# Gate and up by Strassen's algorithm in two token halves, and linear attention in 64-column tiles

## The chip, the cores and the metric

The kernel runs on one core of one Trainium2 chip. The metric is the device time of one launch in microseconds (us). In the profile PE is the matrix engine (TensorE) and PEld its weight loads, DVE is VectorE, ACT is ScalarE, POOL is GpSimd, and SP issues the DMAs. PSUM is the memory that PE writes its sums to, in banks; SBUF is the memory in which all engines' tiles lie.

## The reference

One decoder layer and a last norm, over 1024 prompt tokens and 64 sample tokens (1088 together), model width 1024 and a feed-forward width of 2816, all in float32:

```python
def decoder_layer(x, s0, k_buf, v_buf, w_in, w_gup, b_g, g_mix, g_gla, w_out,
                  g_ffn, w_fg, w_fu, w_fd):
...
    mix = jnp.concatenate([o_g, o_s.reshape(B, T, -1).astype(x.dtype)], axis=-1) @ w_out
    h = x + mix
    hn = rmsnorm(h, g_ffn)
    y = h + (jax.nn.silu(hn @ w_fg) * (hn @ w_fu)) @ w_fd
```

o_g comes from four heads of gated linear attention, chunk after chunk with a state S (64x128 per head). o_s comes from eight heads of dilated windowed attention. y then gets a last rmsnorm.

## The kernel before, in words

Every large product is made from float32 operands that are split in two (L171 on ACT makes the high part, L172 on DVE the low part: raw minus high). One product is then three matmuls per 128x128 block of weights: high by high, high by low, low by high (mm3, L200 to L202). Activations lie transposed, features on the 128 partitions and tokens along the row, and the 1088 tokens are worked on in three chunks, CHUNKS, of 384, 384 and 320. So nearly all of PE's work is matmuls of 128x128 weights by 384 or 320 columns.

The program is ordered by a scheduler: weight loads and their splits are marked high priority and go ahead on their engines, everything else stands where the code puts it. Each engine takes its own instructions strictly in order.

In the order of time: the mixing norm, the input projection with both kinds of attention beside it (0 to about 712 us in the profile), the second half of the out-projection (rows 512 on of `w_out`, the windowed heads; to about 778 us), the feed-forward part (to about 1571 us), and the last norm and output.

- Linear attention: two heads lie in one tile. For each 128 tokens and each head, one matmul makes A by V (L665) and a second adds decayed query by state S (L668). The second has 64 rows of weights, as a head's state is 64 wide.
- Out-projection, second half: `os` loads the attention output of a chunk, 512 rows, from DRAM in one DMA (oraw), and ACT and DVE split it. For each of eight output tiles f and three chunks: the residual with the first half's sum (xa) comes from DRAM, 12 matmuls, an add on DVE into h, a split of h times the norm's gain into hhi and hlo, a square on ACT and a sum on POOL (L1032).
- The norm: the squares are summed over partitions by matmuls with one column (L1038), DVE makes 1/sqrt by small instructions, and it is spread to `rstd_bc` by transposes (L1043 to L1048). Gate and up don't wait for it: `rstd_bc` is multiplied in after their matmuls (L1066, L1068).
- Feed-forward: 22 tiles f of 128 columns. `ff_up(f)` loads and splits 512 KB of gate and of up weights, and for each chunk makes 24 matmuls for gate and 24 for up; DVE, ACT (Silu, L1067), DVE, POOL (L1069) and the split of L171/L172 make ghi and glo. `ff_down` runs once for two tiles f: for each chunk and each of eight output tiles k, 6 matmuls and an add on DVE into h (L1090). So PE makes 3168 matmuls for gate and up, 1584 for down, and 288 for the out-projection's half.
- The tail (L1095 on): the last `ff_down` of each chunk, then transposes, squares, 1/sqrt, and the rows y go out.

Of the kernel before, what the change touches and what calls it, by code (L numbers as in the profile page):

```python
# [102 lines left out]
def hymba_layer(  # L103
# [1103 lines left out]
```

## Time and profile before

| | us |
|---|---|
| runs without the profiler: 1588.16, 1580.25, 1589.38; median | 1588.16 |
| the profiled execution | 1588.28 |
| its span, first to last instruction | 1586.4 |
| PE busy | 1522.2 |
| DVE busy | 717.3 |
| ACT busy | 435.6 |
| POOL busy | 272.1 |

A span is what the profiler saw between the first and the last instruction; 1.9 us of the execution lie around it. An engine is busy while one of its instructions runs. Matmuls overlap in the pipeline, so what one costs is read from the distance between the starts of two of them, and not from its own duration.

### The profile page before, as it was taken

The numbers are of one execution on the slowest core, as the hardware profiler recorded it, in microseconds if no ns is written. First come the engines' busy times: TensorE is split into PE (matmuls) and PEld (weight loads), VectorE is DVE, ScalarE is ACT, GpSimd is POOL, SyncE is SP. The second block draws the span as 40 slices with busy tenths as digits, with TensorE's granted clock in tenths as the row PEclk, the third lists the DMA queues.
The fourth block names the chain that finished last, engine by engine and source line by source line (L and its number), as shares of the span: only waits on it lengthen the run. The fifth ranks groups of instructions, "written<-read, shape, count | busy, mean of one in ns | idle before, by whom it ended". The sixth has DMA issues, their size and how long they took to land.

```text
span 1586.4 us, 28631 instructions
## 1 busy us (share of the span) xinstructions
PE 1522.2 (96%) x12080; PEld 1377.2 (87%) x12080; DVE 717.3 (45%) x1556; ACT 435.6 (27%) x867; POOL 272.1 (17%) x296
## 2 busy tenths in 40 slices
PE   7979999999999998997999999999999999999997
PEld 6768877887776765767999999999999999999997
DVE  5486575543323233335643443433443343444437
ACT  4143242144342445314421212121111212121113
POOL 1494342042112010002310001010000001010002
PEclk9988999999999999989999999999999999999998
DMA  5320121163443547545321101110211101120102
GB/s 155 92 78 30 30 69 43 41 188 106 136 112 93 153 118 217 177 138 175 92 74 50 54 27 54 41 54 27 67 40 41 54 27 54 40 63 18 54 1 114
DMA packets 177425, 126.73 MB, mean 80 GB/s; under 512 B 14576, under 2 KB 169104, under 8 KB 177296
## 3 DMA queue, kind: packets, MB, share of 16 engines
q1 hardware_dynamic: 173088, 124.69, 26.4%
q8 instruction: 95, 1.56, 0.4%
q10 hardware_dynamic: 4208, 0.21, 0.2%
q14 instruction: 34, 0.28, 0.1%
HBM read 101.40 MB, written 23.46 MB: 79 GB/s over the span
## 4 chain that ended last, share of the span: by engine, by line
PE 86%; DMA 5%; DVE 5%; POOL 1%; issue 1%; ACT 1%; SPq 0%; DVEq 0%; ACTq 0%; POOLq 0%
PE ps_mm L200 13%; PE ps_mm L201 12%; PE ps_mm L202 12%; PE ps_S L202 5%; PE ps_S L201 5%; PE ps_S L200 5%; PE ps_T L201 2%; PE ps_T L200 2%; PE ps_T L202 2%; PE ps_S L835 2%; DMA oraw<-o_dram 2%; PE ps_T L933 2%; PE ps_X L977 2%; PE ps_A L202 1%; PE ps_A L200 1%; PE ps_A L201 1%
## 5 line engine op out<-in xcount | busy, mean ns | idle before, releaser
L200 PE MATMUL ps_mm<-xhi,whi 128*128 128x384 f32 (+1 forms) x576 | 199.5, 347 | 2.0 <-ACT whi L171 1.6
L202 PE MATMUL ps_mm<-xhi,wlo 128*128 128x384 f32 (+1 forms) x576 | 194.6, 339 | 1.1 <-DVE wlo L172 1.1
L201 PE MATMUL ps_mm<-xlo,whi 128*128 128x384 f32 (+1 forms) x576 | 194.8, 339 | 0.2 <-DVE xlo L277 0.2
L1069 POOL TENSOR_TENSOR gt<-gt,ut 128x384 f32<-128x384 f32 (+1 forms) x66 | 64.9, 984 | 698.1 <-DVE ut L1068 698.1
L200 PE MATMUL ps_mm<-hhi,whi 128*128 128x384 f32 (+1 forms) x528 | 172.8, 327 | 1.2 <-DVE gt L1066 1.2
L202 PE MATMUL ps_mm<-hhi,wlo 128*128 128x384 f32 (+1 forms) x528 | 173.0, 328 | 0.0
L201 PE MATMUL ps_mm<-hlo,whi 128*128 128x384 f32 (+1 forms) x528 | 172.8, 327 | 0.0
L200 PE MATMUL ps_S<-hhi,whi 128*128 128x384 f32 (+1 forms) x528 | 172.7, 327 | 0.0
L201 PE MATMUL ps_S<-hlo,whi 128*128 128x384 f32 (+1 forms) x528 | 172.7, 327 | 0.0
L202 PE MATMUL ps_S<-hhi,wlo 128*128 128x384 f32 (+1 forms) x528 | 172.5, 327 | 0.0
L200 PEld LDWEIGHTS ps_mm<-xhi,whi 128*128 128x128 f32 x576 | 110.2, 192 | 13.6 <-issue 7.6
L202 PEld LDWEIGHTS ps_mm<-xhi,wlo 128*128 128x128 f32 x576 | 110.2, 191 | 7.3 <-issue 4.8
L201 PEld LDWEIGHTS ps_mm<-xlo,whi 128*128 128x128 f32 x576 | 110.4, 192 | 5.5 <-issue 4.0
L1067 ACT ACTIVATE gt<-gt 128x384 f32<-128x384 f32 (+1 forms) x66 | 33.1, 502 | 294.6 <-DVE gt L1066 294.6
L1068 DVE TENSOR_TENSOR ut<-ps_S,rstd_bc 128x384 f32<-128x384 f32 (+1 forms) x66 | 35.4, 536 | 159.7 <-PE ps_S L202 159.7
L200 PEld LDWEIGHTS ps_mm<-hhi,whi 128*128 128x128 f32 x528 | 99.2, 188 | 1.4 <-DVE gt L1066 1.4
L201 PEld LDWEIGHTS ps_S<-hlo,whi 128*128 128x128 f32 x528 | 99.2, 188 | 0.0
L202 PEld LDWEIGHTS ps_mm<-hhi,wlo 128*128 128x128 f32 x528 | 99.2, 188 | 0.0
L202 PEld LDWEIGHTS ps_S<-hhi,wlo 128*128 128x128 f32 x528 | 99.2, 188 | 0.0
L200 PEld LDWEIGHTS ps_S<-hhi,whi 128*128 128x128 f32 x528 | 99.2, 188 | 0.0
L201 PEld LDWEIGHTS ps_mm<-hlo,whi 128*128 128x128 f32 x528 | 99.2, 188 | 0.0
L1090 DVE TENSOR_TENSOR h<-h,ps_T 128x384 f32<-128x384 f32 (+1 forms) x120 | 63.5, 529 | 68.1 <-PE ps_T L202 68.1
(335 smaller groups left out, 3048.4 us busy)
## 6 DMA issues: line engine op xcount, KB each, us to landing
wraw<-in_w_in_dram SPq DMA_DIRECT2D x22, 512.0 KB, 3.8
wraw<-in_w_ffn_gate_dram SPq DMA_DIRECT2D x22, 512.0 KB, 3.7
wd_raw<-in_w_ffn_down_dram SPq DMA_DIRECT2D x22, 512.0 KB, 3.2
wuraw<-in_w_ffn_up_dram SPq DMA_DIRECT2D x22, 512.0 KB, 3.7
raw<-in_cache_swa_k_dram SPq DMA_DIRECT2D x32, 256.0 KB, 5.4
raw<-in_cache_swa_v_dram SPq DMA_DIRECT2D x32, 256.0 KB, 4.4
xa<-x_dram SPq DMA_DIRECT2D x32, 192.0 KB, 2.6
xr<-in_x_prompt_dram SPq DMA_DIRECT2D x8, 512.0 KB, 8.4
```

The lines of the kernel that those rows point to most:

```text
L200: mm(out=ps, lhsT=whi[k], rhs=xhi[k], start=first and k == 0, stop=False)
L201: mm(out=ps, lhsT=whi[k], rhs=xlo[k], start=False, stop=False)
L202: mm(out=ps, lhsT=wlo[k], rhs=xhi[k], start=False, stop=last and k == n - 1)
L835: ins = mm(out=out, lhsT=qres[own, qi * P + 32 * r : qi * P + 32 * r + 32], rhs=rhs, start=True, stop=True)
L933: nc.tensor.transpose(out=ps[:, r * P : (r + 1) * P], in_=raw[:, r, :], identity=ident)
L977: mm(out=av[rs, b2 * P : (b2 + 1) * P], lhsT=pT[:, t, rs], rhs=vts[b2][:, r, :], start=False, stop=t == 5 and b2 == 1)
L1067: act(out=gt, in_=gt, func=AF.Silu)
L1068: vec.tensor_tensor(out=ut, in0=pu[:, :n], in1=rstd_bc[:, cs], op=ALU.mult)
L1069: pool.tensor_tensor(out=gt, in0=gt, in1=ut, op=ALU.mult)
L1090: vec.tensor_tensor(out=h[:, k, cs], in0=h[:, k, cs], in1=ps[:, :n], op=ALU.add)
```

## The change

Four things change.

1. In linear attention the matmuls of L665 and L668 are cut into 64-column tiles: four for A by V, then four for query by state, where there were two and two, in an order in which neighbours use other parts of the array.
2. The out-projection's second half runs in two token halves of 544, each in two blocks of NH = 272 columns. The first half's h stays in SBUF; the second half's is added into xa and stored back to DRAM, to be read again later. After each half come the sums and `rstd_bc` as before (`out_half`).
3. Gate and up are made by the Strassen-Winograd scheme. The contraction (1024) and the output columns are each cut in two, the tokens of a half too, and seven block products M1 to M7 stand where a plain product has eight. Operands for it: `norm_half` normalises x (now with `rstd_bc` multiplied in first), POOL makes four differences T of 272 columns for each of four pairs of feature tiles, and x blocks and T are split (`operand`). Of the weights POOL makes the four sums S1 to S4, 128x1024 each, and seven blocks are split where there were four. The weights of each pair of f tiles are loaded twice, once per token half. After the products DVE adds the parts together (`after`), and ACT and POOL or DVE make Silu times up.
4. Down stays plain, in blocks of 272 with adds of 544 columns on DVE. The first token half's final rows (five tiles of up to 128 tokens) are made while the second half's first pair is under way (`final_rows`), and then the second half's h is loaded. The tail is cut in 224 and 320 tokens.

PE now makes 3696 matmuls for gate and up, 2112 for down and 384 for the out-projection, nearly all of 272 columns.

```diff
@@ gla head, per chunk @@
+                    os_ = [bank("AX"[i])[:, :P] for i in range(2)]
                     for i in range(2):
-                        o = bank("AX"[i])[:, :P]
-                        hs = slice(64 * i, 64 * i + 64)
-                        mm(out=o, lhsT=AT[:, i * ncmb + c, :], rhs=V[part][:, c, i * P : (i + 1) * P],
-                           start=True, stop=S is None)
-                        if S is not None:
-                            mm(out=o, lhsT=qE[hs, c * P : c * P + P], rhs=S[hs, :], start=False, stop=True)
+                        for ts in halves:
+                            mm(out=os_[i][ts], lhsT=AT[:, i * ncmb + c, ts], rhs=V[part][:, c, i * P : (i + 1) * P],
+                               start=True, stop=S is None)
+                    for ts in halves if S is not None else ():
+                        for i, hs in enumerate(halves):
+                            mm(out=os_[i][ts], lhsT=qE[hs, c * P + ts.start : c * P + ts.stop], rhs=S[hs, :], start=False, stop=True)
+                    for i, o in enumerate(os_):
@@ out-projection, second half, and norm @@
+NH = TT // 4
...
+    def load_rows(c0):
+        hi = outp.tile([P, 4, NH], F32R, tag="ohi", name="ohi", bufs=4)
+        lo = outp.tile([P, 4, NH], F32R, tag="olo", name="olo", bufs=4)
+        for k in range(0, 4, 2):
+            oraw = outp.tile([P, 2, NH], F32, tag="oraw", name="oraw", bufs=3)
+            dma(out=oraw, in_=o_dram[512 + k * P : 512 + (k + 2) * P, c0 : c0 + NH].rearrange("(k p) t -> p k t", p=P))
+            split(hi[:, k : k + 2], lo[:, k : k + 2], oraw)
+        return [hi[:, k] for k in range(4)], [lo[:, k] for k in range(4)]
+    def out_half(hf):
+        os = [load_rows(2 * NH * hf + NH * n) for n in range(2)]
+        sq_acc = outp.tile([P, 2 * NH], F32, tag="acc", name="acc", bufs=2)
+        for f in range(KT):
+            if f % 2 == 0:
+                ws = load_w_out(f, 1)
+            for n in range(2):
+                cs = slice(NH * n, NH * n + NH)
+                xs = x_dram[:, f, 2 * NH * hf + NH * n : 2 * NH * hf + NH * n + NH]
+                xa = outp.tile([P, NH], F32, tag="xa", name="xa", bufs=3)
+                dma(out=xa, in_=xs)
+                ps = bank("mm")[:, :NH]
+                mm3(ps, ws[f % 2], os[n])
+                row = xa if hf else h[0][:, f, cs]
+                vec.tensor_tensor(out=row, in0=ps, in1=xa, op=ALU.add)
+                if hf:
+                    dma(out=xs, in_=xa)
+                if f == 0:
+                    act(out=sq_acc[:, cs], in_=row, func=AF.Square)
+                else:
+                    sq = outp.tile([P, NH], F32, tag="sq", name="sq", bufs=2)
+                    act(out=sq, in_=row, func=AF.Square)
+                    pool.tensor_tensor(out=sq_acc[:, cs], in0=sq_acc[:, cs], in1=sq, op=ALU.add)
...
@@ gate and up @@
+    ORDER = (("M1", "A11", 0, "a", True), ("M6", "S2", 4, "b", True), ("M5", "S1", 3, "c", True), ("M7", "S3", 5, "b", False),
+             ("M2", "A12", 1, "a", False), ("M3", "S4", 2, "c", False), ("M4", "A22", 6, "b", False))
+    def blocks(src, w):
+        raw = {}
+        turn = [0]
+        def room(name):
+            t = raw[name] = ffp.tile([P, KT * P], F32, tag="raw", name="raw", bufs=7)[:, :w]
...
+        for name, m, k in (("A11", 0, 0), ("A21", 1, 0), ("A22", 1, 1), ("A12", 0, 1)):
+            src(room(name), m, k)
+        add = lambda out, a, b, op: pool.tensor_tensor(out=out, in0=raw[a], in1=raw[b], op=op)
+        add(room("S1"), "A21", "A22", ALU.add)
+        add(raw["A21"], "A11", "A21", ALU.subtract)
+        raw["S3"] = raw["A21"]
+        add(room("S2"), "S1", "A11", ALU.subtract)
...
+            if name == "S4":
+                add(raw["S2"], "A12", "S2", ALU.subtract)
+                raw["S4"] = raw["S2"]
...
+        for name, block, slot, bk, first in ORDER:
+            with tc.high_priority():
+                hi, lo = (view(part) for part in parts(block))
+            if bk not in banks:
+                banks[bk] = psum2.tile([P, 2, 512], F32, tag=bk, name=f"ps_{bk}", bufs=2 if bk == "b" else 1)[:, :, :NH]
+            for s in range(2):
+                for k in range(nk):
+                    xhi, xlo = x(k, slot)
+                    one = lambda l, r, i: mm(out=banks[bk][:, s], lhsT=l[:, k, s], rhs=r, start=first and k == 0 and i == 0,
+                                             stop=k == nk - 1 and i == 2, skip_group_check=not first)
+                    one(hi, xhi, 0)
+                    one(hi, xlo, 1)
+                    one(lo, xhi, 2)
+            after(name, banks)
...
+    def operand(pl, B, tag):
+        t = ffp.tile([P, 4, NH], F32, tag="T", name="T", bufs=1)
+        sub = lambda out, a, b: pool.tensor_tensor(out=out, in0=a, in1=b, op=ALU.subtract)
+        sub(t[:, 0], B[:, 3], B[:, 0])
+        sub(t[:, 2], B[:, 2], B[:, 3])
+        sub(t[:, 1], B[:, 2], t[:, 0])
+        sub(t[:, 3], B[:, 1], t[:, 1])
+        hi, lo = (pl.tile([P, 7, NH], F32R, tag=f"{tag}{part}", name=f"{tag}{part}", bufs=4 if tag == "x" else 3) for part in ("hi", "lo"))
+        split(hi[:, 0:3], lo[:, 0:3], B[:, 0:3])
+        split(hi[:, 3:7], lo[:, 3:7], t)
+        return hi, lo
+    def norm_half(hf):
+        t0 = 2 * NH * hf
+        xs = []
+        for k in range(0, KT, 2):
+            B = new_block()
+            for j, v in ((0, B[:, 0:4:3]), (1, B[:, 1:3])):
+                if hf:
+                    dma(out=v, in_=x_dram[:, k + j, t0 : t0 + 2 * NH].rearrange("p (n t) -> p n t", t=NH))
+                vec.scalar_tensor_tensor(
+                    out=v, in0=v if hf else h[0][:, k + j].rearrange("p (n t) -> p n t", t=NH), scalar=gf[:, k + j : k + j + 1],
+                    in1=rstd_bc[:, t0 : t0 + 2 * NH].rearrange("p (n t) -> p n t", t=NH), op0=ALU.mult, op1=ALU.mult)
+            xs.append(operand(bx, B, "x"))
+        return xs
...
+        def made(slot, c, eng):
+            act(out=B[:, slot], in_=c[:, 0], func=AF.Silu)
+            eng.tensor_tensor(out=B[:, slot], in0=B[:, slot], in1=c[:, 1], op=ALU.mult)
+        def after(name, ps):
+            add = lambda out, a, b: vec.tensor_tensor(out=out, in0=a, in1=ps[b], op=ALU.add)
+            if name == "M1":
+                act(out=s1, in_=ps["a"], func=AF.Copy)
+            elif name == "M6":
+                add(u2, s1, "b")
+            elif name == "M5":
+                add(v5, s1, "c")
+            elif name == "M7":
+                add(v5, v5, "b")
+                made(2, v5, pool)
+            elif name == "M2":
+                made(0, ps["a"], vec)
+            elif name == "M3":
+                add(u2, u2, "c")
...
+                add(s1, s1, "b")
+                made(1, s1, pool)
...
@@ down, rows, main loop @@
+    def down(ws, g, h):
+        for k in range(KT):
+            ks = slice(k * P, k * P + P)
+            tag = "abcb"[k % 4]
+            ps = psum2.tile([P, 2, 512], F32, tag=tag, name="ps_d", bufs=2 if tag == "b" else 1)[:, :, :NH]
+            for n in range(2):
+                mm3(ps[:, n], [[w[part][:, ks] for w in ws] for part in range(2)],
+                    [[part[:, j, n * NH : n * NH + NH] for j in range(2)] for part in g])
+            hk = h[:, k].rearrange("p (n t) -> p n t", t=NH)
+            vec.tensor_tensor(out=hk, in0=hk, in1=ps, op=ALU.add)
...
+        ps = psum2.tile([P, 2, 512], F32, tag="b", name="ps_y", bufs=2)
+        y = wpool.tile([P, KT, P], F32, tag="wraw", name="y", bufs=1).rearrange("p (f k) c -> p f (k c)", f=2)
+        c0 = t0 - 2 * NH * hf
+        for k in range(KT):
+            nc.tensor.transpose(out=ps[:m, k // 4, k % 4 * P : k % 4 * P + P], in_=h[hf][:, k, c0 : c0 + m], identity=ident)
+        act(out=y[:m], in_=ps[:m], func=AF.Square, accum_out=st[:m, 0:1])
+        rms(st[:, 1:2], st[:, 0:1], D, st[:, 2:3])
+        vec.scalar_tensor_tensor(out=y[:m], in0=ps[:m], scalar=st[:m, 1:2], in1=gfin[:m].rearrange("p (f c) -> p f c", f=2),
+                                 op0=ALU.mult, op1=ALU.mult)
+        dma(out=out_rows(t0, m), in_=y[:m].rearrange("p f c -> p (f c)"))
...
+    g = None
+    for hf in range(2):
+        for i in range(NF // 2):
+            B = gate_up(i, xs)
+            before, g = g, plain(B)
+            if hf == 0 and i == NF // 2 - 1:
+                xs = norm_half(1)
+            if before:
+                down(ws, before, h[hf])
+            ws = load_down(i)
+            if hf == 0 and i == NF // 2 - 1:
+                down(ws, g, h[0])
+                g = None
+            if hf and i == 0:
+                for t0 in range(0, 2 * NH, P):
+                    final_rows(0, t0, min(P, 2 * NH - t0))
+                h[1] = residual()
+                dma(out=h[1], in_=x_dram[:, :, 2 * NH :])
```

How instructions stand now, at two places. The first is DVE in the feed-forward part. Before, for one pair of tiles f (a weight split is `wlo`, an add after down is L1090):

```order
L1066 TENSOR_TENSOR gt<-ps_mm,rstd_bc 128x320
L172 TENSOR_TENSOR wlo<-wraw,whi 128x1024
L1068 TENSOR_TENSOR ut<-ps_S,rstd_bc 128x320
L172 TENSOR_TENSOR wlo<-wuraw,whi 128x1024
L1090 TENSOR_TENSOR h<-h,ps_T 128x384
L172 TENSOR_TENSOR glo<-gt,ghi 128x320
L172 TENSOR_TENSOR wdlo<-wd_raw,wdhi 128x1024
L1066 TENSOR_TENSOR gt<-ps_mm,rstd_bc 128x384
L1068 TENSOR_TENSOR ut<-ps_S,rstd_bc 128x384
L172 TENSOR_TENSOR glo<-gt,ghi 128x384
```

After, from the last add of one pair's Strassen products (s) to the next pair's first (u), line numbers of the changed kernel (L173 is the low split, L1186 the adds of `after`, L1235 those of `down`):

```order
L1186 TENSOR_TENSOR s_9930<-s_9930,ps_b 128x544
L173 TENSOR_TENSOR glo<-B,ghi 128x544
L173 TENSOR_TENSOR wlo<-raw,whi 128x1024
L1235 TENSOR_TENSOR h<-h,ps_d 128x544 x3
L173 TENSOR_TENSOR glo<-B,ghi 128x544
L1235 TENSOR_TENSOR h<-h,ps_d 128x544 x5
L173 TENSOR_TENSOR wdlo<-raw,wdhi 128x1024 x2
L173 TENSOR_TENSOR wlo<-raw,whi 128x1024
L1186 TENSOR_TENSOR u_10296<-s_10295,ps_b 128x544
L173 TENSOR_TENSOR wlo<-raw,whi 128x1024
```

Before, a pair of f tiles has six weight splits and multiplies and adds in chunks; now three weight splits of the next pair, the split of g and the adds of down stand between the last add of one pair and the first of the next.

The second place is POOL between the out-projection and the first pair of tiles f. Before:

```order
L1032 TENSOR_TENSOR acc<-acc,sq 128x384 x2
L1032 TENSOR_TENSOR acc<-acc,sq 128x320
L1069 TENSOR_TENSOR gt<-gt,ut 128x384 x2
L1069 TENSOR_TENSOR gt<-gt,ut 128x320
L1069 TENSOR_TENSOR gt<-gt,ut 128x384 x2
```

After, from the first half's last sum of squares on (L1053 the sums, L1146 the differences T, L1092 the weight sums S):

```order
L1146 TENSOR_TENSOR T<-B 128x272 x2
L1146 TENSOR_TENSOR T<-B,T 128x272 x2
L1053 TENSOR_TENSOR acc<-acc,sq 128x272 x3
L1146 TENSOR_TENSOR T<-B 128x272 x2
L1053 TENSOR_TENSOR acc<-acc,sq 128x272
L1146 TENSOR_TENSOR T<-B,T 128x272
L1053 TENSOR_TENSOR acc<-acc,sq 128x272 x2
L1146 TENSOR_TENSOR T<-B,T 128x272
L1053 TENSOR_TENSOR acc<-acc,sq 128x272 x3
L1146 TENSOR_TENSOR T<-B 128x272 x2
L1146 TENSOR_TENSOR T<-B,T 128x272
L1092 TENSOR_TENSOR raw<-raw 128x1024
```

The differences of the first half's x, which its products wait for, alternate with the second half's sums of squares, and a weight sum stands between the last of them.

## Rows read from the trace of the kernel before

**Rows 1.** The page: busy us of each engine, share of the span, instructions.

```profile
PE 1522.2 (96%) x12080; PEld 1377.2 (87%) x12080; DVE 717.3 (45%) x1556; ACT 435.6 (27%) x867; POOL 272.1 (17%) x296
```

**Rows 2.** Windows: length, busy us (instructions) of PE, PEld, DVE, ACT, POOL; clock, DMA share, GB/s.

```profile
800.00:900.00 100.00, 100.00 (x612) 100.00 (x611) 40.35 (x65) 20.14 (x31) 10.65 (x10) 1.00 0.15 45
...
720.00:730.00 10.00, 3.27 (x18) 2.94 (x18) 4.14 (x9) 3.77 (x9) 0.00 (x0) 0.86 0.72 236
730.00:740.00 10.00, 10.00 (x51) 10.00 (x52) 4.97 (x11) 4.20 (x10) 1.25 (x2) 0.80 0.16 45
...
780.00:790.00 10.00, 8.54 (x55) 7.92 (x55) 6.58 (x21) 1.05 (x3) 0.00 (x0) 1.00 0.18 52
```

**Rows 3.** Timeline, PE: start us, duration us; ends of two runs of equal matmuls.

```profile
995.51 0.34 PE L202 MATMUL ps_A<-ghi,wdlo 128*128 128x384 f32 x1
...
1013.96 0.33 PE L202 MATMUL ps_X<-ghi,wdlo 128*128 128x384 f32 x1
...
1059.62 0.31 PE L200 MATMUL ps_mm<-hhi,whi 128*128 128x320 f32 x1
...
1066.51 0.31 PE L202 MATMUL ps_S<-hhi,wlo 128*128 128x320 f32 x1
```

**Rows 4.** Timeline of weight loads: six for one-column matmuls, and one of the feed-forward part.

```profile
777.91 0.81 PEld L1038 LDWEIGHTS ps_A<-ones,acc 128*128 128x128 f32 x6
...
1113.24 0.19 PEld L201 LDWEIGHTS ps_mm<-hlo,whi 128*128 128x128 f32 x1
```

**Rows 5.** The critical chain, 700 to 800 us: start us, us on the chain, what.

```profile
720.79 8.60 DMA oraw<-o_dram
```

**Rows 6.** Groups by line and shape, 800 to 1500 us: count, busy us, mean ns, idle before.

```profile
L1069 POOL TENSOR_TENSOR gt<-gt,ut 128x384 f32<-128x384 f32 x41 | 41.7, 1016 | 514.3 <-DVE ut L1068 514.3
L1090 DVE TENSOR_TENSOR h<-h,ps_T 128x384 f32<-128x384 f32 x75 | 41.2, 549 | 40.8 <-PE ps_T L202 40.8
L172 DVE TENSOR_TENSOR wlo<-wuraw,whi 128x1024 fp32r<-128x1024 f32 x21 | 32.3, 1540 | 4.6 <-ACT whi L171 4.6
L172 DVE TENSOR_TENSOR wlo<-wraw,whi 128x1024 fp32r<-128x1024 f32 x20 | 24.5, 1225 | 9.0 <-ACT whi L171 9.0
L172 DVE TENSOR_TENSOR glo<-gt,ghi 128x384 fp32r<-128x384 f32 x42 | 23.5, 559 | 72.7 <-ACT ghi L171 72.7
L1090 DVE TENSOR_TENSOR h<-h,ps_T 128x320 f32<-128x320 f32 x36 | 17.6, 488 | 20.5 <-PE ps_T L202 20.5
```

**Rows 7.** One line's instructions, POOL's scaling of weights: ns min/median/max, first and last start.

```profile
L180 POOL TENSOR_TENSOR wraw<-wraw,gm x22: 1897/1899/2155, 6.8 to 513.7; 128x1024 f32<-128x1024 f32 x22
```

**Rows 8.** Timeline of POOL and DVE around 1114 us: a weight split beside a POOL multiply.

```profile
1113.57 0.88 POOL L1069 TENSOR_TENSOR gt<-gt,ut 128x320 f32<-128x320 f32 x1 [5.95 <-DVE ut L1068]
...
1113.86 1.67 DVE L172 TENSOR_TENSOR wlo<-wuraw,whi 128x1024 fp32r<-128x1024 f32 x1 [0.46 <-ACT whi L171]
```

**Rows 9.** Timeline of DVE in the norm: the chain of small instructions to `rstd_bc`.

```profile
782.53 0.17 DVE L161 TENSOR_SCALAR st<-st 128x9 f32<-128x9 f32 x1
782.74 0.17 DVE L152 TENSOR_SCALAR st<-st 128x9 int32<-128x9 int32 x1
...
788.37 1.01 DVE L1066 TENSOR_TENSOR gt<-ps_mm,rstd_bc 128x384 f32<-128x384 f32 x2
```

**Rows 10.** Scaling of the final rows on DVE (512 columns), one line: ns min/median/max.

```profile
L1171 DVE SCALAR_TENSOR_TENSOR y<-ps_S,st,gfin x2: 741/742/743, 1559.3 to 1574.6; 128x512 f32<-128x512 f32 x2
```

**Rows 11.** Squares of the final rows on ACT (512 columns), timeline.

```profile
1563.01 0.59 ACT L1114 ACTIVATE y<-ps_S 128x512 f32<-128x512 f32 x1
```

**Rows 12.** DMA issues: count, KB each, median us from issue to landing.

```profile
xa<-x_dram SPq DMA_DIRECT2D x32, 192.0 KB, 2.6
...
out_dram<-y SPq DMA_DIRECT2D x8, 512.0 KB, 2.8
...
x_dram<-xa SPq DMA_DIRECT2D x16, 192.0 KB, 4.2
```

**Rows 13.** Linear attention, query by state: ns min/median/max of one line.

```profile
L668 PE MATMUL ps_A<-S,qE x28: 272/322/373, 136.5 to 287.9; 64*128 64x128 f32 x28
```

More of the change, by code (lines that the diff above doesn't have):

```diff
@@ L1042, in hymba_layer @@
-    rows = outp.tile([P, NTT + 1, P], F32, name="rows")
-    vec.tensor_copy(out=rows, in_=st[:, 1, :].unsqueeze(2).broadcast_to([P, NTT + 1, P]))
-    rb = [bank(tag)[:, :n] for tag, (_, n) in zip("ATT", CHUNKS)]
-    for c, j, t, m in tiles:
-        nc.tensor.transpose(out=rb[c][:, j * P : j * P + m], in_=rows[:m, t, :], identity=ident[:m, :m])
-    for c, (c0, n) in enumerate(CHUNKS):
-        vec.tensor_copy(out=rstd_bc[:, c0 : c0 + n], in_=rb[c])
-    outp.release()
-    ffp = open_pool("ffn", side="left")
@@ new lines, in load_down, with plain @@
+    def load_down(i):
+        ws = []
+        for f in (2 * i, 2 * i + 1):
+            with tc.high_priority():
+                raw = ffp.tile([P, KT * P], F32, tag="raw", name="raw", bufs=7)
+                dma(out=raw, in_=w_fd[f * P : (f + 1) * P, :])
+                ws.append([bh.tile([P, D], F32R, tag=f"wd{part}", name=f"wd{part}", bufs=3) for part in ("hi", "lo")])
+                split(*ws[-1], raw)
+        return ws
+    def plain(B):
+        hi, lo = (bh.tile([P, 2, 2 * NH], F32R, tag=f"g{part}", name=f"g{part}", bufs=2) for part in ("hi", "lo"))
+        for k, b in ((0, B[:, 0:4:3]), (1, B[:, 1:3])):
+            split(*(t[:, k].rearrange("p (n t) -> p n t", t=NH) for t in (hi, lo)), b)
+        return hi, lo
@@ new lines, in hymba_layer @@
+    for t, (t0, n) in enumerate(TAIL):
+        c0 = t0 - 2 * NH
+        cs = slice(c0, c0 + n)
+        for k in range(0, KT, 2):
+            ks = [slice(kk * P, kk * P + P) for kk in (k, k + 1)]
+            ps = psum2.tile([P, 2, 512], F32, tag="b", name="ps_d", bufs=2)
+            for j in range(2):
+                mm3(ps[:, j, :n], [[w[part][:, ks[j]] for w in wd] for part in range(2)], [[g[:, i, cs] for i in range(2)] for g in whole])
+            vec.tensor_tensor(out=h[1][:, k : k + 2, cs], in0=h[1][:, k : k + 2, cs], in1=ps[:, :, :n], op=ALU.add)
+            if t:
+                finish(k, c0, n)
+                finish(k + 1, c0, n)
+        rows = [(j * P, min(P, n - j * P)) for j in range(-(-n // P))]
+        if t == 0:
+            for j, m in rows:
+                final_rows(1, t0 + j, m)
@@ new lines, in hymba_layer @@
+    st = fin.tile([P, 12], F32, name="st_last")
+    vec.memset(st, 1.0)
+    sums = psum2.tile([P, 2, 512], F32, tag="b", name="sums", bufs=2)
+    for j in range(3):
+        for part in (acc, last):
+            mm(out=sums[:, 0, j : j + 1], lhsT=part[:, j * P : j * P + P], rhs=one, start=part is acc, stop=part is last)
+    vec.tensor_copy(out=st[:, 0:3], in_=sums[:, 0, 0:3])
+    ps = [psum2.tile([P, 2, 512], F32, tag=tag, name="ps_y", bufs=2 if tag == "b" else 1) for tag in "acb"]
+    for half in range(2):
+        for j, m in rows:
+            for k in range(4):
+                nc.tensor.transpose(out=ps[j // P][:m, half, k * P : k * P + P], in_=h[1][:, 4 * half + k, c0 + j : c0 + j + m], identity=ident)
```

223 lines of the change are left out of this document (88 added, 135 removed).

## The prediction

> **What bounds the kernel now.** I read the busy times first. PE is busy 1522 of 1586.4 us, DVE 717, ACT 436, POOL 272 [rows 1]. Then the windows: in the feed-forward part PE is busy all the time at full clock, DVE 40%, POOL 11% [rows 2]. So there the time is the number of matmuls times the distance between two starts, and the other engines have slack. Elsewhere PE waits in a few places; around the out-projection's start it is busy 3.27 of 10 us, and in the norm behind it 8.54 of 10 [rows 2].
>
> The timeline gives the distances. 107 matmuls of 384 columns follow each other from 995.51 to 1013.96: 18.45/106 = 0.1741 us each. 48 of 320 columns go from 1059.62 to 1066.51: 6.89/47 = 0.1466 us [rows 3]. A column costs (0.1741 - 0.1466)/64 = 0.43 ns.
>
> **The sum is made against the profiled execution**, 1588.3 us (span 1586.4 and 1.9 around it), which is the median (1588.16) to 0.1 us. Runs spread by 9 us, so differences under 1% can't be told from no change.
>
> **1. The matmul stream.** A matmul of 272 columns is not in the trace. By the line through the two rows it costs 0.1466 - 48 x 0.00043 = 0.126 us. Bounds: 0.124, the distance at which six weight loads follow each other when their matmuls have one column only, (0.81 - 0.19)/5 [rows 4], and 0.1466, the shortest that the rows show for a long matmul. I take 0.126: the two rows differ by their columns alone, and the loads by themselves can follow a little faster than that.
> Before: gate, up and down are 1584 triples of chunks (4752 matmuls) at 2 x 0.1741 + 0.1466 = 0.4948 us: 783.8 us. The out-projection's half: 96 triples, 47.5 us. Together 831.3.
> After: 3696 + 2112 + 384 = 6192 at 0.126: 780.2 us. **Term: -51.1 us.** Gate and up have 7/8 of the columns that they had; down and the out-projection have the same columns in shorter pieces, and pay the fixed part of a start more often.
>
> Weight loads are the doubtful point. PEld is busy 100% too [rows 2], one load takes 0.19 us [rows 4]. The Trainium skill (Perfetto Trace Analysis, section Identifying the Most-Contended Engine) says that the busy share of the weight loads tells better than that of the matmuls how near PE is to its limit. By that PE has nothing to give below 0.19 us a matmul, and 6192 of them would take 1176 us. The rows speak against it: matmuls of 320 columns start every 0.1466 us, with a load of 0.19 us each, so loads overlap.
>
> **2. Linear attention.** 56 matmuls at L668 of 0.322 us median, 18 us in all [rows 13], and as many at L665. Twice as many of half the weights' width: if neighbours run side by side, up to half of L668's time goes (-9), if not, the fixed parts add (+5). PE waits for others there in part. **Taken: -3.**
>
> **3. Start of the out-projection.** PE waits for the third chunk's oraw, 8.6 us on the chain [rows 5]. Now the first half needs 1.1 MB in four loads, where all of 2.2 MB was wanted, but weight loads stand ahead on SP. Bounds -6 (most of the 6.7 idle us) to +5. **Taken: -3.**
>
> **4. Start of the feed-forward part.** Before, gate and up start without the norm, and 1.5 us are lost [rows 2]. Now x has to be scaled by `rstd_bc`, turned into differences and split before any product; only the second half's out-projection lies beside it: 192 x 0.126 = 24.2 us, and M1 needs no differences, 3 us more. DVE has, from the end of the first half: the chain to `rstd_bc`, 5.8 us (782.53 to 788.37) [rows 9]; eight scalings of 544 columns at 0.79 (0.742 for 512) [rows 10], 6.3; splits of 816 and 1088 columns four times, by 1.225 for 1024 [rows 6] 0.98 + 1.30, 9.1; 16 adds of 272 columns at 0.44 (0.549 and 0.488 at 384 and 320) [rows 6], 7.0; four weight splits of the out-projection, 4.9; four splits of attention outputs at 0.76 (0.559 for 384) [rows 6], 3.0; two of gate weights, 2.5. Sum 38.6, against 27.2 of PE. Also xa now has a load, an add and a store in three buffers; a load lands in 2.6 us and a store in 4.2 [rows 12], over 7 us for three blocks that PE makes in 4.5, so PE waits in the same stretch anyway. About 11.4 lost, 1.5 were lost before. Bounds 3 to 18, the upper with POOL late too: 16 differences and 16 sums at 0.78 (1.016 for 384, 0.88 for 320) [rows 6, 8] alternate in its queue, 25 us. **Taken: +10.**
>
> **5. Change of halves.** After the last product of half 0 the new x blocks need the old ones' place. PE has two downs, 2 x 96 x 0.126 = 24.2 us, and M1. DVE has: add and splits of the last pair 2.2, scalings 6.3, splits 9.1, 16 adds of 544 at 0.70 (by the same line as 0.44) 11.2, five weight splits 6.1: 35 against 27. One buffer for T makes POOL's four differences (3.1 us) and their split (1.3) take turns. Bounds 2 to 18. **Taken: +9.**
>
> **6. First half's final rows.** There is one buffer y. A row tile takes: square of 1024 columns 1.1 (0.59 for 512) [rows 11], 13 small DVE instructions at 0.2 (starts 782.53 and 782.74) [rows 9] 2.6, scaling 1.5 (0.742 for 512) [rows 10], store 2.8 [rows 12]: 8.0 us. M6 of the second pair needs a PSUM buffer that the fourth tile frees. From the second tile's transposes (eight weight loads, 1.0) that is 1.0 + 3 x 8.0 - 2.8 = 22.2 us; PE has M1, M5, M3 (9.1) and three such groups of transposes (3.0) beside it: 10.1 us lost. Bounds 4 (stores and small instructions half hidden) to 14 (each tile's small instructions behind a weight split on DVE). **Taken: +10.**
>
> **7. Steady pairs.** In each of about 20 pairs PE has 264 x 0.126 = 33.3 us. DVE has nine splits of 1.225, two of 0.76, thirteen adds of 0.70, and one of 0.44: 22.1. POOL has four weight sums and three multiplies of 272. The weight sum is between 1.90 (128x1024 with a spread operand) [rows 7] and 2.4 (line through 0.88 and 1.016); I take 2.1, so 4 x 2.1 + 3 x 0.78 = 10.8. ACT was busy for 20% in such a window [rows 2] and stays far from full. All fit. But POOL and DVE hinder each other: the split beside a POOL multiply took 1.67 us [rows 8], and such splits 1.54 in the mean, where the others took 1.225 [rows 6]: 0.3 to 0.45 late for 0.59 of overlap. The chain with the least slack is M3's and M4's end, POOL's weight sum for the next pair, its split, the add of `s`, the adds of down that free PSUM for down's fifth tile; in the order of DVE's rows I find 0.7 us of slack there. Nothing late if POOL's work falls between, up to 1.5 if one split blocks and is blocked. **Taken: +5** (0.25 a pair), bounds 0 and 30.
>
> The Trainium skill (SBUF — State Buffer, section Who interferes with whom) makes this a lock: a DVE instruction with two SBUF inputs and a GpSimd instruction that reads SBUF exclude each other for their whole length. The trace agrees, with the 0.45 us above. By the rule only DVE's eleven splits (12.5 us a pair) are open to it, and at worst the whole of POOL's time is added to DVE's; that is the second rival below.
>
> **8. Clock.** After the wait at 720 the granted clock is 0.80 for 10 us [rows 2], 2 us of PE's time. Three new waits (4, 5, 6): at most 6. **Taken: +4.** The tail is cut otherwise but works the same columns; I take 0, bounds -3 and +4.
>
> Sum: -51.1 - 3 - 3 + 10 + 9 + 10 + 5 + 4 = -19.1. **1588.3 - 19.1 = 1569 us.**
>
> **Rivals.** *The waits are hidden:* 4, 5 and 6 at their lower ends, 7 at 0, clock +1: 1588.3 - 51.1 - 6 + 3 + 2 + 4 + 1 = 1541. For it: DVE has 60% free in the feed-forward part, and the scheduler pulls weight work ahead. Against: y and T have one buffer each, and DVE's sum in 4 and 5 is over PE's without any waiting.
> *DVE and POOL become the bound of each pair:* one mechanism, the lateness of part 7 [rows 8]: in the worst case POOL's 10.8 us stand on top of DVE's 22.1, 32.9 of PE's 33.3, and every hand-over from ACT to DVE to PE is late. Without part 7 the sum is -24.1; so the change stops paying at 1.2 us lost a pair, and is 1% slower at 2.0. At 2.5 a pair (a weight sum caught behind two splits): 1588.3 - 24.1 + 50 = 1614. For it: the split of 1.67 us. Against: POOL works a third of the time, and weights are split a product ahead, so that most of the lateness falls into slack.
> *Weight loads are the floor:* 0.1466 a matmul: 6192 x 0.1466 = 907.7, that is +76 instead of -51: 1696. Against it: one-column matmuls show loads every 0.124 us [rows 4].
>
> **Chances.** Forecast (waits as summed, 1556 to 1588) 0.57, hidden waits 0.22, DVE and POOL 0.18, weight loads 0.03. The range 1541 to 1606 takes in the first rival and half of the second. Faster by over 1% means under 1572.3: the first rival and 0.33 of the forecast's 0.57, 0.55. Slower by over 1% (over 1604): most of the second rival and the third, 0.18. Within 1%: 0.27.
>
> **What would show it.** Matmuls of 272 columns starting every 0.126 us confirm 1; 0.14 or more breaks it. In the feed-forward part PE's windows should be full but at three places, each some 10 us: ahead of the first M6 (waiting for POOL's or DVE's part of x), at the change of halves, and ahead of the second pair's M6 in half 1 (waiting for `y`). Splits of 1.5 us and more, with PE waiting for `h` or `wlo` in every pair, would show the second rival. A PE that is full throughout shows the first.

## The result and the profile after

The changed kernel takes 1656.07 us (median of 4 runs, 1653.37 to 1657.82) against 1588.77: ratio 1.042, interval 1.0395 to 1.045. It is slower, by 67 us, where 19 us less was forecast. The profiled execution has a span of 1655.2 us, 68.8 more than before.

Busy time of each engine, from the page of the changed kernel, beside [rows 1]:

```profile
PE 1502.5 (91%) x13363; PEld 1345.0 (81%) x13363; DVE 996.3 (60%) x1673; ACT 582.8 (35%) x1007; POOL 556.2 (34%) x419
```

PE has 20 us less busy time and 69 us more span. DVE and POOL have 279 and 284 us more. Windows of 100 us, with the columns of [rows 2]: around the out-projection, in steady pairs, and at the change of halves:

```profile
700.00:800.00 100.00, 66.49 (x475) 63.12 (x471) 61.99 (x111) 35.73 (x59) 51.91 (x48) 0.87 0.56 173
...
900.00:1000.00 100.00, 95.17 (x742) 94.52 (x740) 69.27 (x67) 36.76 (x48) 42.48 (x21) 0.98 0.30 90
...
1200.00:1300.00 100.00, 78.51 (x570) 74.76 (x569) 77.02 (x126) 33.78 (x46) 38.70 (x22) 0.91 0.35 114
```

PE is no longer full in any window of 100 us of the feed-forward part. But the matmuls are as short as forecast. Timeline of PE, both ends of a run of 311 matmuls of 272 columns:

```profile
1574.09 0.29 PE L202 MATMUL ps_d<-glo,wdhi 128*128 128x272 f32 x1
...
1613.01 0.29 PE L203 MATMUL ps_d<-ghi,wdlo 128*128 128x272 f32 x1
```

38.92 us over 310 steps is 0.1256 us each, where [rows 3] gave 0.126.

The span can be cut where the first product of each pair of f tiles starts (first matmul into `ps_a`); "work" is the count of matmuls by 0.1256:

| stage | work | measured | against work or before |
|---|---|---|---|
| start to first gate and up matmul: 775.6 before, 801.5 after | | | +25.9 |
| feed-forward matmuls, 783.8 before | 729.5 | | -54.3 |
| 18 pairs at a steady place (22.3; 329.2; 283.8 us) | 584.8 | 635.3 | +50.5 |
| change of halves, pair 10 to 11 | 45.2 | 54.6 | +9.4 |
| first pairs of half 1, with the final rows | 54.3 | 88.6 | +34.3 |
| last pair's first product to the end, and the tail: 27.0 beyond work before, 30.0 after | 45.2 | 75.2 | +3.0 |
| sum | | | +68.8 |

**A steady pair** takes 36.3 us in half 0 (eight pairs from 862.7 to 1153.0) and 36.0 in half 1 (seven from 1328.1 to 1580.0), for 33.2 of matmuls. Its critical chain (start us, us on the chain, what), from the weight sums of the next pair to PE's first matmul that waited:

```profile
1024.20 5.75 POOL raw L1092 x2
1029.96 0.02 issue
1029.98 1.07 ACT whi L172
1031.05 0.02 issue
1031.07 1.23 DVE wlo L173
1032.30 0.63 DVE s L1186
1032.93 2.42 DVE glo L173
1035.35 1.71 DVE wlo L173
1037.06 0.64 DVE h L1235
1037.70 0.04 issue
1037.74 0.39 PE ps_d L201
```

PE isn't on the chain for 13.5 us. Two sums on POOL take 5.75 us, and a split of 544 columns takes 2.42. The timeline of POOL and of DVE shows what stood beside that split:

```profile
1032.38 2.39 POOL L1092 TENSOR_TENSOR raw<-raw 128x1024 f32<-128x1024 f32 x1 [1.69 <-DVE wlo L173]
1034.72 1.25 POOL L1183 TENSOR_TENSOR B<-B,s 128x272 f32<-128x272 f32 x1
...
1032.85 2.50 DVE L173 TENSOR_TENSOR glo<-B,ghi 128x544 fp32r<-128x544 f32 x1
1035.27 1.79 DVE L173 TENSOR_TENSOR wlo<-raw,whi 128x1024 fp32r<-128x1024 f32 x1
```

The split of g begins 0.47 us after POOL's sum and ends 0.6 us after the sum's end: it got next to nothing done beside it. The weight split behind it loses 0.56 us to POOL's multiply. So the adds of down come late, and PE waits 1.9 us for a PSUM bank. After some of these waits the granted clock is at the lower of its two levels for a while. Windows of 2 us around such a wait, one pair earlier:

```profile
998.00:1000.00 2.00, 1.01 (x9) 0.80 (x7) 2.00 (x2) 0.66 (x1) 1.14 (x1) 1.00 0.00 0
1000.00:1002.00 2.00, 1.09 (x8) 1.09 (x9) 2.00 (x4) 0.00 (x0) 0.00 (x0) 1.00 0.31 63
1002.00:1004.00 2.00, 2.00 (x11) 2.00 (x10) 2.00 (x4) 0.00 (x0) 0.00 (x0) 0.50 0.49 199
1004.00:1006.00 2.00, 2.00 (x13) 2.00 (x12) 0.27 (x2) 0.00 (x0) 0.00 (x0) 0.64 0.00 0
1006.00:1008.00 2.00, 2.00 (x18) 2.00 (x17) 1.19 (x2) 0.00 (x0) 0.00 (x0) 1.00 0.00 0
```

From 1002 to 1006 us 20 matmuls start where full speed starts 32, so 1.5 us of work are lost (the counts in the rows take in matmuls that overlap an edge). The wait of the next pair is as long, and no such fall follows:

```profile
1038.00:1040.00 2.00, 2.00 (x18) 2.00 (x18) 2.00 (x4) 0.00 (x0) 0.00 (x0) 1.00 0.75 260
```

Waits of 1.9 us stand in eight pairs of half 0 and seven of half 1; five and three of them are followed by the fall. Those pairs take 36.9 us, the others 35.3.

**Before the first product**, the chain runs through POOL, where the differences T alternate with sums of squares and a weight sum:

```profile
784.44 0.86 POOL acc L1053
785.30 1.57 POOL T L1146 x2
...
788.44 0.75 POOL T L1146
789.19 2.30 POOL raw L1092
791.49 0.73 POOL T L1146
792.24 1.12 ACT xhi L172
793.38 1.29 DVE xlo L173
...
799.24 0.83 DVE rows L1065
...
801.53 4.35 PE ps_a L1129 x24
```

**In the rows' stretch** it runs through small DVE instructions that take 2 us, and the stores of `y`:

```profile
1222.36 2.29 DVE st L158
...
1245.69 3.63 DMA out_dram<-y
...
1254.17 4.53 DMA out_dram<-y
...
1263.67 5.34 PE ps_b L1129 x24
```

### The profile page after: what moved, and what is told of

Its sections match the earlier page's. It is cut to its first block, busy times and chain, and to the rows that moved or that the text cites. A ratio compares the mean times of both kernels' runs of the same rounds, so it can differ in the third digit from the quotient of the medians.

```text
span 1655.2 us, 32304 instructions
## 1 busy us (share of the span) xinstructions
PE 1502.5 (91%) x13363; PEld 1345.0 (81%) x13363; DVE 996.3 (60%) x1673; ACT 582.8 (35%) x1007; POOL 556.2 (34%) x419
## 4 chain that ended last, share of the span: by engine, by line
PE 54%; DVE 19%; POOL 12%; DMA 6%; issue 4%; ACT 4%; SPq 0%; DVEq 0%; POOLq 0%; ACTq 0%
POOL raw L1092 9%; PE ps_mm L201 7%; PE ps_mm L203 6%; PE ps_mm L202 6%; DVE wlo L173 5%; PE ps_b L1129 4%; PE ps_a L1129 4%; PE ps_c L1129 3%; PE ps_d L201 3%; DVE glo L173 3%; PE ps_d L203 3%; PE ps_d L202 3%; ACT whi L172 3%; PE ps_S L840 2%; PE ps_T L938 2%
## 5 line engine op out<-in xcount | busy, mean ns | idle before, releaser
L1092 POOL TENSOR_TENSOR raw<-raw 128x1024 f32<-128x1024 f32 x88 | 233.6, 2663 | 517.2 <-DVE wlo L173 378.3
L173 DVE TENSOR_TENSOR wlo<-raw,whi 128x1024 fp32r<-128x1024 f32 x154 | 231.6, 1504 | 106.2 <-ACT whi L172 106.1
L201 PE MATMUL ps_d<-ghi,wdhi 128*128 128x272 f32 (+2 forms) x704 | 214.1, 304 | 46.5 <-DVE h L1235 37.0
L172 ACT ACTIVATE whi<-raw 128x1024 fp32r<-128x1024 f32 x154 | 162.8, 1058 | 202.7 <-issue 84.1
L203 PE MATMUL ps_d<-ghi,wdlo 128*128 128x272 f32 (+2 forms) x704 | 210.8, 300 | 1.1 <-DVE wdlo L173 1.1
L202 PE MATMUL ps_d<-glo,wdhi 128*128 128x272 f32 (+2 forms) x704 | 211.0, 300 | 0.0
L1129 PE MATMUL ps_b<-xhi,whi 128*128 128x272 f32 x528 | 153.6, 291 | 9.1 <-DVE y L1261 7.8
L1129 PE MATMUL ps_b<-xhi,wlo 128*128 128x272 f32 x528 | 153.2, 290 | 0.8 <-DVE wlo L173 0.8
L1129 PE MATMUL ps_b<-xlo,whi 128*128 128x272 f32 x528 | 152.7, 289 | 0.3 <-DVE xlo L173 0.3
L1235 DVE TENSOR_TENSOR h<-h,ps_d 128x544 f32<-128x544 f32 x168 | 115.5, 713 | 47.6 <-PE ps_d L203 47.3
L202 PEld LDWEIGHTS ps_d<-glo,wdhi 128*128 128x128 f32 x704 | 140.8, 200 | 0.0
```

The costliest lines, as they stand in the source:

```text
L172: a = by.tensor_copy(out=hi, in_=raw) if by else act(out=hi, in_=raw, func=AF.Copy)
L173: return a, vec.tensor_tensor(out=lo, in0=raw, in1=hi.bitcast(F32), op=ALU.subtract)
L201: mm(out=ps, lhsT=whi[k], rhs=xhi[k], start=first and k == 0, stop=False)
L202: mm(out=ps, lhsT=whi[k], rhs=xlo[k], start=False, stop=False)
L203: mm(out=ps, lhsT=wlo[k], rhs=xhi[k], start=False, stop=last and k == n - 1)
L1092: add = lambda out, a, b, op: pool.tensor_tensor(out=out, in0=raw[a], in1=raw[b], op=op)
```

## The experiments

The theory after reading this: DVE instructions with two inputs in SBUF (splits, the small ones of 1/sqrt, scalings) and POOL's two-input work exclude each other. In the pairs that costs the 50 us; in the other two places it adds to single buffers. The rival: DVE has too much to do, or POOL's sums are too long.

| run | edit | us (runs) | ratio to before, interval |
|---|---|---|---|
| the change | | 1656.1 (4) | 1.042, 1.0395 to 1.045 |
| e1_sums_dve | weight sums on DVE | 1602.9 (4) | 1.008, 1.006 to 1.011 |
| e5_pool_writes_only | fills for sums | 1590.5 (8) | 1.000, 0.997 to 1.002 |
| e8_s2_dve | S2 alone on DVE | 1621.5 (2) | 1.017, 1.012 to 1.022 |
| e4_no_rows | final rows left out | 1630.6 (2) | 1.026, 1.021 to 1.030 |
| g1_gla_only | before, 64-column tiles | 1581.9 (10) | 0.995, 0.993 to 0.997 |
| f1_defer | e1, norm of half 1 later | 1604.1 (2) | 1.008, 1.005 to 1.010 |
| f4_defer_y2 | f1, two buffers y | 1586.1 (8) | 0.996, 0.993 to 0.999 |
| f5_f4_diffs_dve | f4, differences on DVE | 1575.6 (4) | 0.990, 0.988 to 0.991 |
| f6_f5_xa | f5, five xa | 1574.3 (4) | 0.989, 0.986 to 0.992 |
| f7_no_defer | f5, norm not moved | 1580.7 (4) | 0.991, 0.988 to 0.995 |
| f8_mults_dve | f5, multiplies on DVE | 1579.2 (4) | 0.991, 0.987 to 0.994 |
| f10_two_steps | f5, norm in two steps | 1576.7 (4) | 0.990, 0.988 to 0.992 |

**Sums on DVE.**

```diff
-        add = lambda out, a, b, op: pool.tensor_tensor(out=out, in0=raw[a], in1=raw[b], op=op)
+        add = lambda out, a, b, op: vec.tensor_tensor(out=out, in0=raw[a], in1=raw[b], op=op)
```

> The changed kernel with its four weight sums per pair (S1 to S4, 128x1024) on DVE instead of POOL. A steady pair takes 36.3 us in the changed kernel (seven pairs from 889.97 to 1144.88), against 33.3 us of matmuls. Theory A, exclusion: two-input DVE splits and POOL's sums hold each other up, and at a pair's end the split of g (2.50 us for 0.71) and the next weight split (1.79 for 1.23) make PE wait 1.9 us, after which its clock is low. Then a pair falls to 33.5 to 34.3 us although DVE has 5 us more to do, and the whole falls by 40 to 55 us, to 1600 to 1616. Theory B, DVE has too much to do: it is busy 68 to 72% and gets 5 us more a pair, so a pair stays at 36 us or gets longer, and the whole stays at 1650 to 1700.

Measured 1602.9, 53 us less. Between the profiled runs it is 54.1 us, and 51.4 of them lie in the 18 pairs (583.9 us for 635.3). A window of this run:

```profile
900.00:1000.00 100.00, 100.00 (x798) 100.00 (x798) 81.19 (x88) 37.95 (x49) 13.31 (x10) 1.00 0.32 96
```

PE is full at full clock, with DVE at 81%: a pair takes 33.2 us, its matmuls alone. DVE's amount of work is not the limit. But a sum is also shorter on DVE (1.33 us) than on POOL, so this run alone doesn't tell exclusion from the length of POOL's sums.

**POOL busy, but not reading.**

```diff
-        add = lambda out, a, b, op: pool.tensor_tensor(out=out, in0=raw[a], in1=raw[b], op=op)
+        def add(out, a, b, op):
+            for part in (out, out, out[:, :512]):
+                pool.memset(part, 0.5)
```

> The changed kernel with each weight sum on POOL replaced by three fills of a constant (1024, 1024 and 512 columns), about as long as a sum (0.955 us for 1024 in the kernel before), which write to the same tiles and read nothing; so the Strassen sums of weights are left out of the computation. Theory A1, POOL's reading is what holds DVE up: splits beside the fills stay at 0.71 and 1.23 us, PE's 1.9 us wait in each pair goes, pairs 33.5 to 34.3 us, whole 1600 to 1616. Theory A2, it is the length of POOL's step in the chain of the pair's end, or any work of POOL: pairs stay near 36 us and the whole near 1656.

Groups by line in the pairs from 900 to 1100 us, the changed kernel:

```profile
L1092 POOL TENSOR_TENSOR raw<-raw 128x1024 f32<-128x1024 f32 x23 | 60.8, 2656 | 131.4 <-DVE wlo L173 131.4
L173 DVE TENSOR_TENSOR wlo<-raw,whi 128x1024 fp32r<-128x1024 f32 x40 | 60.7, 1517 | 32.3 <-ACT whi L172 32.3
...
L173 DVE TENSOR_TENSOR glo<-B,ghi 128x544 fp32r<-128x544 f32 x10 | 16.1, 1610 | 0.0
```

and with the fills:

```profile
L1094 POOL MEMSET raw<- 128x1024 f32 (+1 forms) x74 | 60.2, 816 | 102.9 <-DMA raw<-in_w_ffn_up_dram 65.3 <-DVE wlo L173 35.2
...
L173 DVE TENSOR_TENSOR wlo<-raw,whi 128x1024 fp32r<-128x1024 f32 x42 | 51.5, 1225 | 25.2 <-ACT whi L172 25.2
...
L173 DVE TENSOR_TENSOR glo<-B,ghi 128x544 fp32r<-128x544 f32 x12 | 8.7, 722 | 0.6
```

POOL is busy as long with the fills (60.2 us) as with the sums (60.8), and DVE's splits go back to 1.225 and 0.72 us. At a pair's end a fill stands where the sum stood:

```profile
975.65 1.97 POOL L1094 MEMSET raw<- 128x1024 f32 x2
...
976.46 0.72 DVE L173 TENSOR_TENSOR glo<-B,ghi 128x544 fp32r<-128x544 f32 x1
977.38 1.23 DVE L173 TENSOR_TENSOR wlo<-raw,whi 128x1024 fp32r<-128x1024 f32 x1 [0.20 <-ACT whi L172]
```

Pairs take 33.2 us. 1590.5 is lower than expected: the second pair of half 1, with the rows in it, takes 56.1 us where e1_sums_dve has 69.5. What holds DVE up is that POOL reads, not that it works or how long. (The fills don't wait for each other's inputs, so a part of the chain is looser too, and how much of the 50 us went by that isn't shown; but DVE's durations don't depend on it.) The Trainium skill (SBUF — State Buffer, section Who interferes with whom) says that only a GpSimd instruction that reads SBUF contends with DVE's second input; both runs agree.

**One sum of the four.**

```diff
-        add(room("S2"), "S1", "A11", ALU.subtract)
+        vec.tensor_tensor(out=room("S2"), in0=raw["S1"], in1=raw["A11"], op=ALU.subtract)
```

> The changed kernel with only the sum S2 on DVE; S1, S3 and S4 stay on POOL. S2 is the sum that POOL makes at a pair's end (1032.38 to 1034.77 us in the changed kernel), beside the split of g and the weight split ahead of down's adds. Theory: it is this one overlap that makes PE wait 1.9 us and lose clock, so S2 alone brings most of what all four brought (53 us): 1605 to 1625. Rival: the four sums hold DVE up evenly through the pair, so one of four brings a quarter: 1635 to 1650.

1621.5: two thirds of what all four bring (three quarters by the ratios), and a pair takes 34.3 us. But the expectation took the wrong sum. POOL's order is S1, S3, S2, S4: S2 is the second of the two at 1024.20, and the one beside the split of g is S4. The run's timeline of DVE and POOL still has that overlap:

```profile
988.49 2.21 DVE L173 TENSOR_TENSOR glo<-B,ghi 128x544 fp32r<-128x544 f32 x1 [0.73 <-ACT ghi L172]
990.62 1.79 DVE L173 TENSOR_TENSOR wlo<-raw,whi 128x1024 fp32r<-128x1024 f32 x1
...
987.71 2.41 POOL L1092 TENSOR_TENSOR raw<-raw 128x1024 f32<-128x1024 f32 x1
```

What went is the first half of the chain (S3 and S2, 5.75 us on POOL, then S2's split, and behind it in DVE's queue the add of `s`). PE now waits 0.9 us a pair instead of 1.9, and the granted clock stays at 1.00. So there are two parts: sums that are late by exclusion push `s` back, and the overlap with S4 delays what follows.

**Final rows.**

```diff
-                for t0 in range(0, 2 * NH, P):
-                    final_rows(0, t0, min(P, 2 * NH - t0))
```

> The changed kernel without the five row tiles of the first token half in the second half's first pairs; the final norm and output of 544 tokens are left out. PE waits 3.8 and 7.8 us between 1250 and 1264 us behind the rows' PSUM buffers. Theory: the rows cost these 11.6 us, 4.7 us of their transposes and clock, and 1 to 3 us of waits around: 12 to 20 us less, 1636 to 1644. Rival: the wait only moves, as the reload of h or the weight splits of these pairs are as late: under 6 us less.

1630.6, 25 us less, more than the theory's 20 and than any bound of the prediction. The two first pairs of half 1 take 60.4 us for 88.6. Of these 28 us 23.5 are left in the whole of the profiled runs (1631.7 for 1655.2); the next pair gives 3.5 back (35.4 for 31.9). So most of the wait doesn't move.

**Linear attention alone**, the first part of the diff put on the kernel before:

> The kernel before with the 64-column tiles of linear attention alone. The out-projection's first wait begins at 708.8 us after and at 711.4 before. Theory: the tiles gain these 2.6 us, ratio to before 0.997 to 0.999. Rival: the start of the windowed attention or the input projection sets that time and the 2.6 us are chance or come from another start of the out-projection: 0.9995 to 1.001.

0.995: more than the theory allowed. The matmuls themselves gave little: the last A by V starts at 288.3 us for 288.7. The rest came later. The chain of this run at the out-projection, for [rows 5]:

```profile
709.42 6.70 DMA oraw<-o_dram
...
716.73 6.67 DMA oraw<-o_dram
```

The second wait was 8.60 us and the first began at 712.59. Why the loads came sooner wasn't tried.

**Norm of half 1 moved, then a second y, then differences on DVE** (each on top of the one before, all with the sums on DVE):

```diff
+            if hf == 0 and i == 1:
+                norm_sums(1, *late_sq)
...
-        y = wpool.tile([P, KT, P], F32, tag="wraw", name="y", bufs=1).rearrange("p (f k) c -> p f (k c)", f=2)
+        pl, tag = ((wpool, "wraw"), (nrm, "scr"))[t0 // P % 2]
+        y = pl.tile([P, KT, P], F32, tag=tag, name="y", bufs=1).rearrange("p (f k) c -> p f (k c)", f=2)
...
-        sub = lambda out, a, b: pool.tensor_tensor(out=out, in0=a, in1=b, op=ALU.subtract)
+        sub = lambda out, a, b: vec.tensor_tensor(out=out, in0=a, in1=b, op=ALU.subtract)
```

> Weight sums on DVE (1602.9 us) and the second token half's sums of squares, 1/sqrt chain and transposes moved behind the second pair's products, in other tiles. With the sums on DVE alone, PE stood from 779.3 to 796.9 us around these one-column matmuls and transposes, 14.5 us of it idle. Theory: the norm of the second half stands in PE's and DVE's order ahead of the first products, so M1 and three quarters of M6 and M5 can now run before the last block of x is split (about 795.6): 5 to 9 us less, 1594 to 1598. Rival: the x blocks themselves are as late (the last one was split at 796.7): 0 to 3 us less.

Nothing gained, 1604.1. The first product starts at 778.7 us for 796.9, the third pair's only 3.5 us earlier, as the x blocks are late, and these 3.5 are given back in the third pair itself, which takes 37.4 us for 33.2.

> As f1_defer, and the final rows' y alternates between two buffers. In the run with the sums on DVE, PE waited 5.9, 8.1 and 5.6 us between 1209 and 1233 us for rows. Theory: the single y and its 2.8 to 4.5 us store between two rows set the pace, so a row takes 5 us for 8 and some 9 to 12 us go, 1583 to 1588. Rival: the small DVE instructions of each row, in one queue with the weight splits, set it: under 4 us less, 1591 or more.

18 us less than f1_defer, more than the 9 to 12 expected: the single y set the pace of the rows. In the profiled runs the pair with the rows takes 54.7 us for 69.6, and the stretch from the last pair's first product to the end, which has rows too, 71.3 for 76.2.

> As f4_defer_y2, and the differences T of x on DVE too, 32 of 128x272, about 0.42 us each for 0.78 and up to 1.6 on POOL. Theory (exclusion): at the first half's start and at the change of halves the four differences of a block take 3.1 us and more on POOL and hold DVE's splits up; on DVE they take 1.7: 4 to 8 us less than f4_defer_y2. Rival (DVE has too much to do there): no gain or up to 5 us more.

10.5 us less than f4, more than expected. The third pair starts 6.3 us earlier (848.3 for 854.6), and the change of halves takes 49.6 us for 54.3. Whether that is exclusion, or that DVE makes a difference in 0.42 us for POOL's 0.78, this run can't tell. This version beats both kernels: 0.990 of before, and the one with linear attention alone has 0.995.

**Variants of it.** More buffers for xa (three to five); the norm put back; multiplies on DVE; the norm in two steps:

```diff
-                xa = outp.tile([P, NH], F32, tag="xa", name="xa", bufs=3)
+                xa = outp.tile([P, NH], F32, tag="xa", name="xa", bufs=5)
...
-                made(2, v5, pool)
+                made(2, v5, vec)
...
-            if hf == 0 and i == 1:
-                norm_sums(1, *late_sq)
+            if hf == 0 and i in (1, 3):
+                norm_sums(1, *late_sq, second=i == 3)
```

> As f5_f4_diffs_dve, with five buffers for xa instead of three. Theory: in the second half of the out-projection load, add and store of xa pace PE (its chain shows xa's DMAs for a third of the time from 755 to 800 us), so 3 to 7 us less than f5_f4_diffs_dve. Rival: the x blocks on DVE end as late anyway: within 2 us of it.

1.3 us less, within the spread: the rival.

> Weight sums and differences of x on DVE, and y in two buffers, but the second half's norm left where the change has it. Theory: with the differences on DVE the x blocks are ready earlier, and now the norm's place ahead of the first products costs 3 to 7 us against the version with it moved (1575.6): 1579 to 1583. Rival: its place costs nothing, as f1_defer showed with the differences on POOL: 1574 to 1577.

5 us more (2 by the ratios, as the two were measured beside other runs of before), but the intervals overlap: inconclusive. In the profiled runs the fourth pair starts 7.1 us later (892.7 for 885.6).

> As f5_f4_diffs_dve, and the three multiplies of Silu and up per pair on DVE too (128x272, 0.42 us for POOL's 0.78). POOL then does nothing in the feed-forward part but fills. Theory (exclusion still costs a little at the change of halves and the rows): 1 to 4 us less, 1571.5 to 1574.5. Rival (DVE, busy 81% in the pairs, is near its limit and gets 1.3 us more): 0 to 10 us more.

3.6 us more, intervals overlap: no gain.

> As f5_f4_diffs_dve, with the second half's moved norm in two steps: sums and 1/sqrt after the second pair's products, transposes and copies two pairs later. In f1_defer, f4 and f5 the third pair takes 37.4 us where the others take 33.2: the 4.2 us that moving the norm brought at the start were given back there. Theory: PE's or DVE's order there waits for the chain of small instructions, and apart the two steps cost 1 us: 2.5 to 4 us less, 1571.5 to 1573. Rival: it is the PSUM buffers that the norm takes from the products, once in each step, so it is given back twice: 1575 or more.

The third pair falls from 37.4 to 34.3 us, as the theory has it, and the fifth pays 0.9. The whole stays at 1576.7, so 2 us that the runs can't tell.

## Why the prediction was wrong

- **Part 1, matmuls:** right. 0.1256 us for 0.126, and 54.3 us less in the feed-forward part. The rival in which weight loads are the floor is out: loads are busy for 0.19 us each and follow each other every 0.1256.
- **Part 7, steady pairs: the step that failed.** "+5 (0.25 a pair)" measured 50.5 over 18 pairs, 2.8 each, beyond its bounds of 30 in all and 1.5 a pair. The chain was named (weight sum, its split, the add of `s`, adds of down), and so was the mechanism [rows 8]. The slack of 0.7 us was worked out with a sum of 2.1 us and a split of g of 0.76, their durations alone; in the pairs they take 2.66 and 1.61. The order shown ahead of the prediction has the split of g and the weight split right in front of down's adds. S4 is written over S2 and waits for S2's split, so it starts just ahead of the split of g, which takes 2.50 to 2.52 us in each of the fifteen pairs that wait 1.9. The overlap was no matter of chance, as "POOL works a third of the time" had it. What the runs show in place of 0.25 a pair is the second rival's mechanism, with 2.5 a pair and 1614, to which 0.18 was given: e1_sums_dve takes the 50.5 us away, and e5_pool_writes_only shows that POOL's reading is what lengthens the splits. The 42 us from 1614 to 1656 are mostly parts 3, 4 and 6.
- **Part 6, rows:** right place and buffer, wrong size: 34 us for 10, or 25 by e4_no_rows. The single y was worth 15 us in this place (f4_defer_y2). A store landed in 3.6 to 4.5 us and not in 2.8 [rows 12]; weights loaded beside it, but that this is why wasn't tried. The 13 small instructions were put at 0.2 us each; beside POOL's sums single ones take 2.3. That this made the stretch long isn't shown: in e1_sums_dve none takes over 0.73, and the two pairs take 91.4 us for 88.6.
- **Parts 3 and 4, up to the first product:** +9.3 forecast (-3, 11.4, and 0.9 for the out-projection's own matmuls), 28.5 measured from the end of attention to the first product (711.4 to 775.6 before, 708.8 to 801.5 after). The upper bound of part 4 spoke of POOL's queue; its mechanism is on the chain, with a weight sum in it, but 28.5 is beyond what the bound of 18 allows. Putting the differences on DVE brought the third pair forward by 6.3 us; the norm's place, which f1_defer tried, did not matter with them on POOL. With the differences on DVE (f5_f4_diffs_dve) the third pair still starts 18 us later than 54.3 us of matmuls after 775.6 would have it. From 768 to 798 us that run's chain is DVE for three quarters, so DVE's own work, as summed in part 4, bears on it, but no run took it away.
- **Part 5, change of halves:** 9.4 for 9, right.
- **Part 2, linear attention:** -8.6 us for -3 by g1_gla_only (by the interval 6 to 12), within its bounds, but not by the mechanism named: 0.4 us are gained by the last A by V, and the rest is luck as far as the forecast goes. How much of it the changed kernel has isn't shown.
- **Part 8, clock:** put at three places; it is also lost behind eight of the fifteen waits of 1.9 us in the pairs, some 1.6 us each (36.9 against 35.3), and was not counted there.

## What to carry to other kernels

Before work is put on POOL because POOL is idle, see what two-input DVE instructions stand beside it in the steady order: the later of the two can take as long as both (2.50 us for 0.71 here), and busy shares (69% DVE, 42% POOL) don't show it. Take a chain's slack with durations as they are beside each other. In this kernel trading columns of matmul for elementwise work paid only once the adds that free PSUM came on time: 54 us of PE's work were gained, and the whole change was worth 16 us (linear attention's share included) only after sums, differences, y and the norm had been moved.

## What was not expected of the hardware

- A split of 128x544 took 2.50 us for 0.71 beside one POOL sum, which began 0.47 us earlier and kept its 2.39. The other way round, a sum that began 1.37 us into a weight split (1026.56 us) took 3.39. The one that starts second waited. A small instruction of DVE on one column took 2.29 us for 0.17. Fills on POOL for the same time lengthened no split; in that run the longest small instruction, 0.73 us, stood beside a multiply of POOL.
- Behind eight of fifteen waits of PE of 1.9 us the granted clock was low (0.50 and 0.64 in two windows of 2 us, shown above); behind the other seven, of the same length, it stayed at 1.00. With waits of 0.9 us in e8_s2_dve it stayed at 1.00 in the steady pairs, and a pair cost 1.2 us over its matmuls.
